# A hybrid attention and gating block on one core: the last query rotation behind the first attention loads, softmax tiles in pools of their own region, an early exponential

## The chip, the cores and the metric

The kernel runs on one core of a Trainium2 chip. The metric is the device time of one execution in microseconds (us); the time of a kernel is the median of its runs. One more execution was recorded by the hardware profiler, and all durations of single instructions are from it. The engines are named as in the profile: PE (TensorE, matrix products), DVE (VectorE), ACT (ScalarE), POOL (GpSimd) and SP (SyncE, which here only issues DMAs). A line number such as L377 is a line of the kernel before.

## The reference

The block has one layer. It normalises x (1024 tokens by 1024 channels), projects it once, and splits the columns into two gated branches; in short:

```python
h = rmsnorm(x, norm_g[l])
q, k, v, za, u, vs, zs, gm = jnp.split(h @ w_in[l], IN_SPLITS, axis=-1)
q = partial_rope(q.reshape(B, S, ATT_HEADS, HEAD_DIM), pos)      # 16 heads of 64, first 16 dims rotated
k = partial_rope(k.reshape(B, S, ATT_KV_HEADS, HEAD_DIM), pos)   # 2 key heads
a = window_sink_attention(q, k, v, att_sinks[l])                 # chunks of 64, window of 3 chunks
a = (a * jax.nn.silu(za)) @ w_att_out[l]
sgo = chunked_spatial_gating(gelu(u), gelu(vs), sg_w[l], sg_b[l], sg_ln_g[l], sg_ln_b[l])
sgo = (sgo * jax.nn.silu(zs)) @ w_sg_out[l]
ga, gs = jnp.split(jax.nn.sigmoid(gm + b_merge[l]), N_BRANCHES, axis=-1)
x = x + (ga * a + gs * sgo) @ w_o[l]
return rmsnorm(x, final_g)
```

Attention takes for each chunk of 64 queries the keys of its own chunk and the two before it. The softmax has one learned sink logit for each head, so the row maximum and the denominator take the sink in.

## The kernel before, in words

All large products run in fp32 by a split of each operand into a high and a low part (fp32r): three products stand for one. A product of two 256-row blocks of output by 1024 columns of tokens is done by a Strassen-like scheme with seven products instead of eight. `gemm_pair` (L351) does one such pair: it takes the forms of the input ("b11", "t1", "t2", "b21", "t3", "b22", "t4") as moving operands and split weights (`ready`) as stationary ones. Each of the seven is a `product` (L334) of 12 matrix instructions of 128x512 at L342. The order in the code is b11, t1, t2, b21, t3, b22, t4. Three banks take the sums: `acc` ("mm") gets b11, t2, t3 and t4 one after the other, so a product with t4 has to wait until the subtraction of L377 has read what t3 left; `t5` ("o") gets t1 and b22.

After each product `gemm_pair` calls a `hook`. Other work is hung on these hooks, a step at a time: that is how attention, rotation and loads come to lie beside the products. `split_next` casts the weights of the next pair on ACT (L155) and takes the rest on DVE (L156); `make_sums` adds weight blocks on DVE (L242 to L245).

The stages that matter here follow one another. Four pairs make the queries q; they go raw to `q_raw` in DRAM (L458) and, scaled and split (`split_q`: ACT L1034, DVE L1036), to `q_hl` by DMAs on SP (L1040). The first 16 of 64 dims of each head have to be rotated: `rotate(g, pause)` (L1083) loads them for eight heads from `q_raw` into tiles "rot" (L1089, four DMAs), multiplies them with tables of cosines and sines on DVE (L1109 to L1116), splits them in tiles "qhl" and stores them to `q_hl` over the plain values (two halves with four DMAs each, L1040). `rope_tables` makes the tables, `rotate_keys` does the same for the keys. `rotate(0, 3)` runs on the hooks of the last query pair, `rotate(1, 1)` on those of the pair after it, the first of the z stage ("z pair").

On the same hooks, behind the rotation, `first_loads` loads keys and queries of the first two attention steps (`query_stage`, L1152 and L1184). Attention itself begins on the first hook of the next pair. There are 32 steps, each of 128 queries by 4 heads. `softmax_stage` (L1212) makes scores on PE (L1230, bank "sc", two of them), row minima on DVE (L1238, L1239; scores carry a negative scale), and exponentials on ACT into a tile "pr" (L1243); the small values lie in tiles "sm". `weight_stage` turns the weights on PE (L1274), `value_stage` multiplies them with the values (L1315). Step 2 of attention loads its queries when the scores of step 0 have been read, as there are two tiles "q".

On-chip memory is taken in pools, stacked. The pool "ahead" is open from before the queries to the end of attention. On it lies "queries" with all tiles of rotation and splitting ("cos", "sin", "wide", "tab", "qhl", "rot"); it is closed behind the z pair, and "attention" with "sm", "pr", "pT", "pTb", "aT" and "vb" takes the same place. A tile of the later pool waits for whatever still uses the place in the earlier one.

The order of instructions on each queue is not that of the code. The framework traces the program, then plans each engine's queue with a cost model of its own; earlier in the code means a higher priority, and an instruction that is ready sooner may go first. `after(second, first)` (L158) adds an order without a wait; `pace[0]` is the last copy that ended a product, `term[0]` the last finished sum. Every queue then runs strictly in the planned order.

The line that hangs up the two jobs is L1197:

```python
steps_of_q += [rotate(1, 1), first_loads()]
gemm_pair(hb, rest(z_dr, 0), part_of_q)
stage.close()
```

Of the kernel before, what the change touches and what calls it, by code (L numbers as in the profile page):

```python
# [24 lines left out]
F32 = mybir.dt.float32  # L25
F32R = mybir.dt.float32r
# [4 lines left out]
P = 128  # L31
# [3 lines left out]
HALF = 512  # L35
# [17 lines left out]
def hybrid_tile(  # L53
# [947 lines left out]
    aheads = ahead.enter_context(tc.tile_pool(name="ahead", bufs=1))  # L1001
    stage = ExitStack()
    pool = stage.enter_context(tc.tile_pool(name="queries", bufs=1))
    SC = -(HD**-0.5)
    tables = []

    def rope_tables():

        cos_sb = mtile([P, NT, 16], F32, "cos", 1, pool)
        sin_sb = mtile([P, NT, 16], F32, "sin", 1, pool)  # L1010
        nc.sync.dma_start(cos_sb[:], cos)
        nc.sync.dma_start(sin_sb[:], sin)
        yield
        for src in (cos_sb[:, :, 0:8], sin_sb[:, :, 8:16]):
            tab = mtile([P, HALF], F32, f"tab{len(tables)}", 1, pool)
            wide = []
            for i in range(4):
                v = mtile([P, 2, 8, 8], F32, "wide", 4, pool)
                nc.vector.tensor_copy(v[:], src[:, i : i + 5 : 4, :].unsqueeze(2).broadcast_to([P, 2, 8, 8]))
                wide.append(v)  # L1020
            yield
            pt = bank("tp")
            for i, v in enumerate(wide):
                nc.tensor.transpose(pt[:, i * P : (i + 1) * P], v[:].rearrange("p a h d -> p (a h d)"), ident[:])
            nc.scalar.copy(tab[:], pt[:])
            tables.append(tab)
            yield

    def split_q(src, places):

        hl = mtile([P, 2, HALF], F32R, "qhl", 3, pool)
        hi, lo = (hl[:, a, :].rearrange("p (t q c) -> p t c q", c=2, q=64) for a in range(2))
        src = src.rearrange("p (t c q) -> p t c q", c=2, q=64)
        nc.scalar.mul(hi, src, SC)  # L1034
        for c in range(2):
            nc.vector.scalar_tensor_tensor(  # L1036
                lo[:, :, c], src[:, :, c], SC, hi[:, :, c].bitcast(F32), op0=ALU.mult, op1=ALU.subtract
            )
        for at, dst in places:
            nc.sync.dma_start(dst, hl[at].bitcast(F32))  # L1040
# [3 lines left out]
    def rotate_keys(pause):  # L1044

        x1, x2, a, b = (mtile([P, HALF], F32, "rot", 5, pool) for _ in range(4))
        for j, dst in enumerate((x1, x2)):
            nc.gpsimd.memset(dst[:], 0.0)  # L1050
            src = k_raw[:].rearrange("(g d) t -> g d t", g=2)[:, 8 * j : 8 * j + 8]
            for half in range(2):
                nc.sync.dma_start(dst[half * 64 : half * 64 + 16], src[:, :, half_of(half)])

        def split_rows(src, j):
            hl = mtile([P, 2, HALF], F32R, "qhl", 3, pool)
            split(hl[:, 0, :], hl[:, 1, :], src)
            for half in range(2):
                for dup in range(2):
                    for g in range(2):  # L1060
                        at = half * 64 + 8 * g
                        nc.gpsimd.dma_start(
                            k_dr[dup * HD + 8 * j : dup * HD + 8 * j + 8, 2 * g : 2 * g + 2, half_of(half)],
                            hl[at : at + 8].bitcast(F32),
                        )

        for _ in range(1 + pause):
            yield
        c, s = tables[0][:], tables[1][:]
        after(nc.vector.tensor_mul(a[:], x1[:], c), term[0])  # L1070
        after(nc.vector.tensor_mul(b[:], x2[:], s), term[0])
        yield
        after(nc.vector.tensor_sub(a[:], a[:], b[:]), term[0])
        split_rows(a[:], 0)
        yield
        after(nc.vector.tensor_mul(x2[:], x2[:], c), term[0])
        after(nc.vector.tensor_mul(x1[:], x1[:], s), term[0])
        yield
        after(nc.vector.tensor_add(x2[:], x2[:], x1[:]), term[0])
        split_rows(x2[:], 1)  # L1080
        yield

    def rotate(g, pause):  # L1083

        x1, x2, a, b = (mtile([P, HALF], F32, "rot", 5, pool) for _ in range(4))
        for j, dst in enumerate((x1, x2)):
            src = q_raw[:].rearrange("(h d) t -> h d t", h=16)[8 * g : 8 * g + 8, 8 * j : 8 * j + 8]
            for half in range(2):
                nc.sync.dma_start(dst[halves[half]], src[:, :, half_of(half)])  # L1089

        def split_rows(src, j):
            split_q(
                src,
                [
                    (
                        (halves[half], a),
                        q_hl[a].rearrange("(h d) t -> h d t", h=16)[
                            8 * g : 8 * g + 8, 8 * j : 8 * j + 8, half_of(half)
                        ],
                    )  # L1100
                    for a in range(2)
                    for half in range(2)
                ],
            )

        for _ in range(1 + pause):
            yield
        c, s = tables[0][:], tables[1][:]
        after(nc.vector.tensor_mul(a[:], x1[:], c), term[0])  # L1109
        after(nc.vector.tensor_mul(b[:], x2[:], s), term[0])  # L1110
        nc.vector.tensor_sub(a[:], a[:], b[:])
        split_rows(a[:], 0)
        yield
        after(nc.vector.tensor_mul(x2[:], x2[:], c), term[0])
        after(nc.vector.tensor_mul(x1[:], x1[:], s), term[0])
        nc.vector.tensor_add(x2[:], x2[:], x1[:])  # L1116
        split_rows(x2[:], 1)
        yield
# [75 lines left out]
            yield  # L1194


    steps_of_q += [rotate(1, 1), first_loads()]  # L1197
    gemm_pair(hb, rest(z_dr, 0), part_of_q)
    stage.close()


    stage = ExitStack()
    pool = stage.enter_context(tc.tile_pool(name="attention", bufs=1))

    def atile(shape, dt, tag, bufs):
        return mtile(shape, dt, tag, bufs, pool)

    def window_of(t, c):

# [2 lines left out]
    def softmax_stage(g, t, par, qt):  # L1212

        kt = keys[g, t][0]
        q_of = qt[:].rearrange("p i (q c) -> p c (i q)", c=2)
        k0 = 0 if t else P
        nmax = atile([P, 2, 2], F32, "sm", 12)
        sums = atile([P, 2, 2], F32, "sm", 12)  # L1220
        pr = atile([P, 2, 384], F32, "pr", 2)
        held_in = {}
        sinks_of = (v[:, 4 * g + par : 4 * g + par + 3 : 2] for v in (sink_sb, nsink_sb))
        sk, nsk = sinks_of
        for c in range(2):
            lo, hi = window_of(t, c)
            sc = bank("sc")[:].rearrange("p (i k) -> p i k", i=2)
            for i in range(2):
                for f in range(2):
                    nc.tensor.matmul(  # L1230
                        sc[:, i, k0:],
                        q_of[:, c, i * P : (i + 1) * P],
                        kt[:, f, k0:],
                        start=f == 0,
                        stop=f == 1,
                    )

            nc.vector.tensor_reduce(nmax[:, c, :], sc[:, :, lo:hi], axis=mybir.AxisListType.X, op=ALU.min)  # L1238
            nc.vector.tensor_tensor(nmax[:, c, :], nmax[:, c, :], nsk, op=ALU.min)  # L1239
            for i in range(2):  # L1240
                at = 192 * c if t else P * (c + 1)
                held_in[c, i] = pr[:, i, at : at + hi - lo]
                nc.scalar.activation(  # L1243
                    held_in[c, i],
                    sc[:, i, lo:hi],
                    AF.Exp,
                    bias=nmax[:, c, i : i + 1],
                    scale=-1.0,
                    accum_out=sums[:, c, i : i + 1],
                )  # L1250
        es = atile([P, 2, 2], F32, "sm", 12)
        nc.vector.tensor_add(es[:], sk.unsqueeze(1).broadcast_to([P, 2, 2]), nmax[:])
        nc.scalar.activation(es[:], es[:], AF.Exp)
        nc.vector.tensor_add(es[:], es[:], sums[:])
        inv = atile([P, 2, 2], F32, "sm", 12)
        nc.vector.reciprocal(inv[:], es[:])
        for c in range(2):
            for i in range(2):
                v = held_in[c, i]
                if c == 0:  # L1260
                    nc.vector.tensor_scalar_mul(v, v, inv[:, c, i : i + 1])
                else:
                    nc.scalar.mul(v, v, inv[:, c, i : i + 1])
        return pr
# [635 lines left out]
```

## Time and profile before

| what | us |
|---|---|
| median of 3 runs | 914.42 |
| lowest and highest | 913.27, 915.49 |
| the profiled execution, as timed | 915.36 |
| its span, first to last instruction | 913.6 |
| PE busy in it | 895.3 |
| DVE, ACT, POOL busy | 696.7, 527.1, 141.9 |

The mean granted clock of PE is 0.995. In rows of a timeline the first number is the start in us from the span's beginning, the second the duration in us (of all instructions that the row merges), then engine, line, operation, tile written and tiles read; in brackets stands how long the engine had been idle before, and what ended that. Rows with a stretch (300.00:320.00) give its length, then for PE, PE's weight loads, DVE, ACT and POOL the busy time and number of instructions, then the granted clock, the DMA engines' share and GB/s. Rows of waits give the sum, the number and the longest. In the chain of waits a row is start, duration and what filled it. "SPq" rows are DMAs being issued, not moved.

### The profile page before, as it was taken

Reading aid. Unit: us, or ns where it says so; the run is one execution under the profiler, and the core shown is the slowest. Engines: PE = TensorE matmul, PEld = TensorE weight load, DVE = VectorE, ACT = ScalarE, POOL = GpSimd, SP = SyncE. Lnnn points to the kernel's source line nnn. Section 1 sums busy time; section 2 is a strip of 40 time slices with the busy share of each in tenths; the row PEclk is TensorE's granted clock in tenths of the full one; section 3 lists DMA queues with packets and bytes.
Section 4 is the critical chain, followed back from the end, with each engine's and each line's share of the span. In section 5 each row is a group of like instructions: output and inputs, shape, how many; then the busy total and the mean of one; then the engine's idle time right before and its main releaser. Section 6 shows DMA issues by size and latency. Waiting matters only on the chain.

```text
span 913.6 us, 13183 instructions
## 1 busy us (share of the span) xinstructions
PE 895.3 (98%) x4284; PEld 745.1 (82%) x4284; DVE 696.7 (76%) x1263; ACT 527.1 (58%) x1058; POOL 141.9 (16%) x204
## 2 busy tenths in 40 slices
PE   8999999999999899999999999999998999999996
PEld 6778888888888788888888888888877887888885
DVE  6869966666685678888878888647797589579996
ACT  6866533334544467677677676664674385367443
POOL 1222222212030001111110111201001111110012
PEclk9999999999999999999999999999999999999999
DMA  9997888958788657878686789899859755998632
GB/s 330 204 248 212 271 203 173 172 158 257 260 258 274 199 167 212 212 153 208 180 227 228 234 240 229 215 338 343 304 195 363 224 201 150 312 304 277 208 117 113
DMA packets 131598, 209.57 MB, mean 229 GB/s; under 512 B 12649, under 2 KB 61033, under 8 KB 131530
## 3 DMA queue, kind: packets, MB, share of 16 engines
q1 hardware_dynamic: 110072, 149.74, 49.7%
q0 software_dynamic: 21312, 58.73, 28.3%
q8 instruction: 34, 0.56, 0.3%
q14 instruction: 34, 0.28, 0.1%
q10 hardware_dynamic: 146, 0.27, 0.1%
HBM read 147.74 MB, written 86.11 MB: 256 GB/s over the span
## 4 chain that ended last, share of the span: by engine, by line
PE 88%; DVE 7%; DMA 2%; issue 1%; ACT 1%; SPq 0%; DVEq 0%; ACTq 0%
PE ps_mm L342 37%; PE ps_o L342 27%; PE ps_sc L1230 3%; PE ps_mm L669 3%; PE ps_tp L342 3%; PE ps_tp L669 2%; PE ps_o L1315 2%; PE ps_sc L342 2%; PE ps_tp L1274 2%; PE ps_o L669 2%; PE ps_tp L917 2%; PE ps_sc L669 1%; DVE bq L185 1%; DVE wl L156 1%; DMA wr<-in_w_dram 1%
## 5 line engine op out<-in xcount | busy, mean ns | idle before, releaser
L155 ACT CAST wh<-s 128x1024 fp32r<-128x1024 f32 (+1 forms) x79 | 79.2, 1005 | 90.2 <-PE ps_mm L342 48.6
L156 DVE TENSOR_TENSOR wl<-wr,wh 128x512 fp32r<-128x512 f32 (+1 forms) x77 | 72.0, 936 | 51.3 <-ACT wh L155 50.7
L156 DVE TENSOR_TENSOR wl<-s,wh 128x1024 fp32r<-128x1024 f32 (+1 forms) x79 | 92.5, 1171 | 10.8 <-ACT wh L155 10.6
L155 ACT CAST wh<-wr 128x512 fp32r<-128x512 f32 (+1 forms) x77 | 63.1, 821 | 62.6 <-PE ps_mm L342 34.2
L342 PE MATMUL ps_o<-T_t1h,wh 128*128 128x512 f32 x148 | 58.9, 398 | 0.8 <-ACT wh L155 0.7
L342 PE MATMUL ps_o<-T_b22h,wh 128*128 128x512 f32 x148 | 58.2, 393 | 0.0
L342 PE MATMUL ps_o<-T_b22l,wh 128*128 128x512 f32 x148 | 57.9, 391 | 0.0
L342 PE MATMUL ps_o<-T_b22h,wl 128*128 128x512 f32 x148 | 57.8, 390 | 0.0
L342 PE MATMUL ps_mm<-T_b11h,wl 128*128 128x512 f32 x140 | 54.9, 392 | 2.8 <-DVE wl L156 2.8
L342 PE MATMUL ps_o<-T_t1h,wl 128*128 128x512 f32 x148 | 57.7, 390 | 0.0
L342 PE MATMUL ps_o<-T_t1l,wh 128*128 128x512 f32 x148 | 57.6, 389 | 0.0
L342 PE MATMUL ps_mm<-T_t4h,wh 128*128 128x512 f32 x140 | 55.5, 397 | 1.2 <-DVE x L377 1.2
L342 PE MATMUL ps_mm<-T_t2h,wl 128*128 128x512 f32 x140 | 55.2, 395 | 0.0
L342 PE MATMUL ps_mm<-T_t3l,wh 128*128 128x512 f32 x140 | 54.6, 390 | 0.6 <-DVE T_t3l L156 0.6
L342 PE MATMUL ps_mm<-T_t2l,wh 128*128 128x512 f32 x140 | 55.2, 394 | 0.0
L342 PE MATMUL ps_mm<-T_t4h,wl 128*128 128x512 f32 x140 | 55.1, 394 | 0.0
L342 PE MATMUL ps_mm<-T_b11h,wh 128*128 128x512 f32 x140 | 55.1, 393 | 0.0
L342 PE MATMUL ps_mm<-T_t4l,wh 128*128 128x512 f32 x140 | 55.0, 393 | 0.0
L342 PE MATMUL ps_mm<-T_t2h,wh 128*128 128x512 f32 x140 | 55.0, 393 | 0.0
L342 PE MATMUL ps_mm<-T_b11l,wh 128*128 128x512 f32 x140 | 54.9, 392 | 0.0
L342 PE MATMUL ps_mm<-T_t3h,wh 128*128 128x512 f32 x140 | 54.9, 392 | 0.0
L1243 ACT ACTIVATE pr<-ps_sc,sm 128x192 f32<-128x192 f32 (+2 forms) x128 | 50.9, 410 | 6.6 <-DVE sm L1239 5.5
(389 smaller groups left out, 2397.4 us busy)
## 6 DMA issues: line engine op xcount, KB each, us to landing
wr<-in_w_dram SPq DMA_DIRECT2D x86, 256.0 KB
sums<-in_w_dram POOLq DMA_DIRECT2D x20, 512.0 KB, 6.5
s<-sums SPq DMA_DIRECT2D x20, 512.0 KB
q_hl<-qhl SPq DMA_DIRECT2D x16, 512.0 KB
q<-q_hl SPq DMA_DIRECT2D x64, 128.0 KB
y_dr<-x POOLq DMA_DIRECT2D x28, 256.0 KB, 6.7
g<-in_w_dram POOLq DMA_DIRECT2D x12, 512.0 KB, 6.7
wr<-in_w_dram SPq DMA_DIRECT2D x11, 512.0 KB
```

The source lines that it names most:

```text
L155: nc.scalar.copy(hi, src)
L156: return nc.vector.tensor_sub(lo, src, hi.bitcast(F32))
L185: op(dst[:, i : i + 2, :], a[:, i : i + 2, :], c[:, i : i + 2, :])
L342: nc.tensor.matmul(acc, lt, rt, start=fresh and k == 0 and n == 0, stop=k == 3 and n == 2, skip_group_check=True,)
L669: mm = nc.tensor.matmul(acc[:], lt, rt, start=fresh and k == 0 and n == 0, stop=k == 3 and n == 2, skip_group_check=True,)
L917: nc.tensor.matmul(pm[:, t * P : (t + 1) * P], xh[:, half * 4 + t, g * P : (g + 1) * P], bias[-1][1][:, g % 4, :], start=True, stop=True,)
L1230: nc.tensor.matmul(sc[:, i, k0:], q_of[:, c, i * P : (i + 1) * P], kt[:, f, k0:], start=f == 0, stop=f == 1,)
L1243: nc.scalar.activation(held_in[c, i], sc[:, i, lo:hi], AF.Exp, bias=nmax[:, c, i : i + 1], scale=-1.0, accum_out=sums[:, c, i : i + 1],)
L1274: nc.tensor.transpose(dst, pr[:, i, block * P : block * P + width], ident[:])
L1315: nc.tensor.matmul(po[:, cs], lt, rt, start=n == 0, stop=n == len(terms) - 1)
```

## The change

Four things change.

1. On the hooks of the z pair `first_loads` comes ahead of `rotate(1, 1)`.
2. An exponential of one column ("warm") is issued ahead of the z pair, ordered behind the last copy of the pair before.
3. The tiles "sm" and every other "pr" move into the pool "ahead"; the others of "pr" go to a pool "weights" that is opened first where "queries" was. The split rows "qhl" get a pool "split" on top of "queries".
4. The cosines, the sines and the spread rows ("wide") that become tables use tiles "rot" (five slots of 128x512) instead of tiles of their own.

```diff
     stage = ExitStack()
     pool = stage.enter_context(tc.tile_pool(name="queries", bufs=1))
+    split_pool = stage.enter_context(tc.tile_pool(name="split", bufs=1))
...
+    def rot_tile():
+        return mtile([P, HALF], F32, "rot", 5, pool)
+
+    both = rot_tile()[:, 0 : 2 * NT * 16].rearrange("p (f t d) -> p f t d", f=2, t=NT)
+
     def rope_tables():
 
-        cos_sb = mtile([P, NT, 16], F32, "cos", 1, pool)
-        sin_sb = mtile([P, NT, 16], F32, "sin", 1, pool)
-        nc.sync.dma_start(cos_sb[:], cos)
-        nc.sync.dma_start(sin_sb[:], sin)
+        for f, src in enumerate((cos, sin)):
+            nc.sync.dma_start(both[:, f], src)
         yield
-        for src in (cos_sb[:, :, 0:8], sin_sb[:, :, 8:16]):
+        for src in (both[:, 0, :, 0:8], both[:, 1, :, 8:16]):
             tab = mtile([P, HALF], F32, f"tab{len(tables)}", 1, pool)
-            wide = []
+            wide = rot_tile()
             for i in range(4):
-                v = mtile([P, 2, 8, 8], F32, "wide", 4, pool)
-                nc.vector.tensor_copy(v[:], src[:, i : i + 5 : 4, :].unsqueeze(2).broadcast_to([P, 2, 8, 8]))
-                wide.append(v)
+                nc.vector.tensor_copy(
+                    wide[:, i * P : (i + 1) * P].rearrange("p (a h d) -> p a h d", a=2, h=8),
+                    src[:, i : i + 5 : 4, :].unsqueeze(2).broadcast_to([P, 2, 8, 8]),
+                )
             yield
             pt = bank("tp")
-            for i, v in enumerate(wide):
-                nc.tensor.transpose(pt[:, i * P : (i + 1) * P], v[:].rearrange("p a h d -> p (a h d)"), ident[:])
+            for i in range(4):
+                nc.tensor.transpose(pt[:, i * P : (i + 1) * P], wide[:, i * P : (i + 1) * P], ident[:])
...
-        hl = mtile([P, 2, HALF], F32R, "qhl", 3, pool)
+        hl = mtile([P, 2, HALF], F32R, "qhl", 3, split_pool)
...
-        x1, x2, a, b = (mtile([P, HALF], F32, "rot", 5, pool) for _ in range(4))
+        x1, x2, a, b = (rot_tile() for _ in range(4))
...
-    steps_of_q += [rotate(1, 1), first_loads()]
+    steps_of_q += [first_loads(), rotate(1, 1)]
+    after(nc.scalar.activation(warm[:], eps_sb[:], AF.Exp), pace[0])
     gemm_pair(hb, rest(z_dr, 0), part_of_q)
     stage.close()
 
 
     stage = ExitStack()
+    weights_pool = stage.enter_context(tc.tile_pool(name="weights", bufs=1))
     pool = stage.enter_context(tc.tile_pool(name="attention", bufs=1))
...
+    n_pr = [0]
+
+    def small():
+        return mtile([P, 2, 2], F32, "sm", 12, aheads)
...
-        nmax = atile([P, 2, 2], F32, "sm", 12)
-        sums = atile([P, 2, 2], F32, "sm", 12)
-        pr = atile([P, 2, 384], F32, "pr", 2)
+        nmax, sums = small(), small()
+        n_pr[0] += 1
+        pr = mtile([P, 2, 384], F32, f"pr{n_pr[0] % 2}", 1, aheads if n_pr[0] % 2 else weights_pool)
...
-        es = atile([P, 2, 2], F32, "sm", 12)
+        es = small()
...
-        inv = atile([P, 2, 2], F32, "sm", 12)
+        inv = small()
```

The same replacements of "qhl" and "rot" are made in `rotate_keys` and `rotate`.

More of the change, by code (lines that the diff above doesn't have):

```diff
@@ L1055, in split_rows @@
         def split_rows(src, j):
-            hl = mtile([P, 2, HALF], F32R, "qhl", 3, pool)
+            hl = mtile([P, 2, HALF], F32R, "qhl", 3, split_pool)
             split(hl[:, 0, :], hl[:, 1, :], src)
@@ L1083, in rotate @@
     def rotate(g, pause):
-        x1, x2, a, b = (mtile([P, HALF], F32, "rot", 5, pool) for _ in range(4))
+        x1, x2, a, b = (rot_tile() for _ in range(4))
         for j, dst in enumerate((x1, x2)):
```

## The prediction

> **What bounds the kernel now.** I read the page first, then the table of TensorE's waits, then the stretches of 20 us.
>
> ```profile
> span 913.6 us, 13183 instructions
> PE 895.3 (98%) x4284; PEld 745.1 (82%) x4284; DVE 696.7 (76%) x1263; ACT 527.1 (58%) x1058; POOL 141.9 (16%) x204
> ```
>
> ```profile
> PE ps_mm L342 <- DVE wl L156: 2.8, 2, 1.7
> ...
> PE ps_sc L1230 <- ACT pr L1243: 1.5, 1, 1.5
> PE ps_mm L342 <- DVE x L377: 1.2, 1, 1.2
> ```
>
> ```profile
> 300.00:320.00 20.00, 17.25 (x76) 13.70 (x75) 13.69 (x35) 9.75 (x28) 0.00 (x0) 0.93 0.70 207
> ...
> 680.00:700.00 20.00, 16.89 (x64) 12.58 (x63) 19.03 (x22) 11.26 (x15) 2.17 (x4) 0.91 0.83 304
> ```
>
> TensorE (PE) is busy 895.3 of 913.6 us, so 18.3 us of waits is all that any reordering can win. The edit touches the stretch 300 to 320: 2.75 us idle there (20.00 less 17.25), and a granted clock of 0.93. Two of the listed waits lie in it, the 1.5 us and the 1.2 us one. The longer of the waits for DVE wl lies in 680 to 700, which the edit does not name. So I argue about these two waits, and about what is late next when they go.
>
> The earlier wait, from the timeline (start, duration, engine, line):
>
> ```profile
> 299.45 0.69 DVE L1109 TENSOR_TENSOR rot<-rot,tab 128x512 f32<-128x512 f32 x1
> 299.53 0.39 PE L342 MATMUL ps_mm<-T_t3h,wl 128*128 128x512 f32 x1
> ...
> 303.60 0.68 DVE L377 TENSOR_TENSOR x<-x,ps_mm 128x512 f32<-128x512 f32 x1
> ...
> 304.20 0.75 DVE L1036 SCALAR_TENSOR_TENSOR qhl<-rot,qhl 128x256 fp32r<-128x256 f32 x2
> ...
> 304.33 0.50 PE L342 MATMUL ps_mm<-T_t4h,wh 128*128 128x512 f32 x1 [1.24 <-DVE x L377]
> ```
>
> The third form's last product ends at 299.92 (299.53 + 0.39). The subtraction that reads it (L377) could start then, but starts at 303.60, because VectorE (DVE) takes the rotation's instructions from L1109 on first. The product with t4 writes the same bank and waits 1.24 us. The stretch of 3 us around it shows VectorE full and PE empty:
>
> ```profile
> 303.00:306.00 3.00, 1.76 (x8) 1.41 (x8) 3.00 (x7) 1.08 (x2) 0.00 (x0) 1.00 0.57 162
> ```
>
> The later wait, where attention begins:
>
> ```profile
> 309.36 1.23 DVE L156 TENSOR_TENSOR wl<-s,wh 128x1024 fp32r<-128x1024 f32 x1 [0.20 <-ACT wh L155]
> 309.45 1.05 PE L1230 MATMUL ps_sc<-k,q 128*128 128x128 f32 x8
> ...
> 312.76 0.62 DVE L1238 TENSOR_REDUCE sm<-ps_sc 128x2 f32<-128x128 f32 x2 [2.18 <-DMA z_dr<-x]
> ...
> 313.46 1.29 SPq L1184 DMA_DIRECT2D q<-q_hl  x2
> ...
> 313.67 1.28 ACT L1243 ACT_TABLE_LOAD   x1 [3.43 <-DMA z_dr<-x]
> ...
> 314.97 0.31 ACT L1243 ACTIVATE pr<-ps_sc,sm 128x64 f32<-128x64 f32 x1
> ...
> 315.72 1.39 PE L1230 MATMUL ps_sc<-k,q 128*128 128x128 f32 x8 [1.49 <-ACT pr L1243]
> ...
> 317.32 0.63 PE L342 MATMUL ps_mm<-T_t2h,wl 128*128 128x512 f32 x1
> ...
> 323.62 0.64 PE L1230 MATMUL ps_sc<-k,q 128*128 128x256 f32 x4
> ```
>
> ```profile
> L1238 DVEq EVENT_SEMAPHORE  x4: 49/50/50, 311.6 to 312.7; - x4
> ```
>
> The first scores are there by 310.5 (309.45 + 1.05). The first row minimum (L1238) starts at 312.76, after VectorE's sequencer has gone through four waiting instructions up to 312.7. The profile names z_dr as releaser, but L1238 reads scores and writes a tile "sm" of the pool "attention", which takes the place of "queries"; there lie the split rows "qhl", still read by eight stores to q_hl, issued until 308.97 (row below). A store there takes about 3.9 us to land, hence 312.7. I take these stores as the true releaser. Then ScalarE (ACT) loads the exponential's table, 1.30 us to its first exponential (314.97 less 313.67), and the second group of scores, which needs a bank back, waits 1.49 us.
>
> The wait costs more than itself:
>
> ```profile
> 317.00:319.00 2.00, 2.00 (x6) 1.54 (x6) 1.10 (x7) 2.00 (x11) 0.00 (x0) 0.53 0.62 134
> 319.00:321.00 2.00, 2.00 (x9) 1.58 (x8) 0.99 (x5) 0.92 (x4) 0.00 (x0) 0.62 0.85 236
> ...
> 694.00:696.00 2.00, 2.00 (x7) 1.52 (x6) 2.00 (x3) 0.00 (x0) 1.08 (x2) 0.50 1.08 395
> ```
>
> ```profile
> 285.78 3.89 DMA q_hl<-qhl
> ...
> 291.72 5.90 DMA wr<-in_w_dram
> ...
> 317.11 3.40 PE ps_mm L342 x8
> 320.51 0.51 PE ps_tp L1274 x4
> ...
> 324.73 2.73 PE ps_mm L342 x12
> 327.46 0.44 PE ps_tp L1274 x4
> ```
>
> Behind it the granted clock is 0.53 and 0.62; in the chain of waits eight products take 3.40 us where twelve take 2.73 later. The same dip stands at 694 to 696, behind the other large wait; none follows the 1.24 us one (clock 1.00 in 303 to 306).
>
> **The change part by part.**
>
> Softmax tiles by region. "sm" and the first step's "pr" move into the pool "ahead", which is open beforehand, and the second step's "pr" takes the front of "queries", where "rot" lies and no store reads. So L1238 no longer waits for stores. Its new start is where VectorE is free: in the profile the last split before it ends at 310.59 (309.36 + 1.23). From L1238's start to ScalarE's 0.91 us (313.67 less 312.76), from the first exponential to the second scores 0.75 (315.72 less 314.97): scores at 310.59 + 0.91 + 0.75 = 312.25. PE gets there at 315.72 less both waits, 312.99. The wait of 1.49 goes, with 0.74 to spare.
>
> The dummy exponential. It moves a load of 1.28 us to behind the copy that ends a product of the pair before.
>
> ```profile
> 277.97 1.05 ACT L155 CAST wh<-wr 128x1024 fp32r<-128x1024 f32 x1 [1.61 <-PE ps_o L342]
> ```
>
> ScalarE idles 1.61 us there; load and a tiny exponential are 1.28 + 0.31 = 1.59. I cost it at nothing. Without that cover it is up to 1.59 us on ScalarE, below zero nothing.
>
> The last quarter behind the first loads. The hooks of the z pair now give the two query stages first, then the rotation's loads (third), a pause, and its two halves (fifth and sixth, instead of third and fourth). Its arithmetic stays: six instructions like L1109 and four of L1036. They are ordered behind the latest finished term, and by the fifth hook that is L377: L377 can start at about 300.7 (behind one split of 1.23 us, like L156 above, begun at 299.45 in L1109's place) and end by 301.4, while t4 is due at 303.09 (304.33 less 1.24). The 1.24 us go. On SP:
>
> ```profile
> 291.72 0.60 SPq L200 DMA_DIRECT2D wr<-in_w_dram  x1
> 293.64 2.86 SPq L1089 DMA_DIRECT2D rot<-q_raw  x4
> 296.55 0.62 SPq L1184 DMA_DIRECT2D q<-q_hl  x1
> ...
> 299.93 1.93 SPq L1184 DMA_DIRECT2D q<-q_hl  x3
> ...
> 303.81 5.16 SPq L1040 DMA_DIRECT2D q_hl<-qhl  x8
> ```
>
> Four query loads (0.62 + 1.93 = 2.55 us of issue) go ahead of the four rotation loads. SP stood from 292.32 to 293.64, so these come at most 2.55 − 1.32 = 1.2 us later, and the last lands by about 301.6 (296.5 + 1.2 + 3.9), when VectorE has just done L377. The eight stores stay at 5.16 us and come no earlier than before.
>
> Tables and "split" pool. The cosines, sines and spread rows use "rot" slots; the same copies and transposes remain.
>
> ```profile
> L1025 ACT COPY tab<-ps_tp x2: 587/588/588, 237.2 to 242.8; 128x512 f32<-128x512 f32 x2
> ...
> L1070 DVE TENSOR_TENSOR rot<-rot,tab x1: 687/687/687, 246.2 to 246.2; 128x512 f32<-128x512 f32 x1
> ```
>
> The key rotation's first product (246.2) may now wait for these slots, free by 243.4 (242.8 + 0.59): nothing, with 2.8 us to spare.
>
> The sum: waits 1.24 + 1.49; the eight slow products 3.40 − 8/12 × 2.73 = 1.58; the slow scores 1.39 − 1.05 = 0.34; the slow transposes 0.51 − 0.44 = 0.07. Together 4.72 us. The profiled execution took 915.36 us (span 913.6) and would take 910.6; the median of the three runs shown is 914.42, 0.94 lower, so 909.7.
>
> Here one rule speaks against the sum. The row: a wait of 1.49 us, then a clock of 0.53. The Trainium skill (TensorE: Matmul & The Clock Gate, "What's actually happening") has the half rate only after an idle window of some 3.4 us. By that rule the dip is not this wait's, and the sum would be 2.73 us. The trace disagrees, with a dip directly behind each of the two large waits, and I sum by the trace.
>
> What I cannot see is the order: the framework plans every queue anew from its own costs (loads written after the eight stores were issued before them, 296.55 against 303.81). The later waits at 680 to 700 may shift either way by their size; I take zero.
>
> **The rivals.**
>
> The third step's queries are late next. Their loads are issued at 313.46 and about 314.1, and land 3.89 to 5.90 us later, 318.0 to 320.0. PE takes these scores at 323.62 now, but would at 323.62 − 4.72 = 318.9. For it: SP issues without a pause from 303.81. Against: four loads have left that stretch. It gives back up to 1.1 us, and with a dip like the one above (1.58 + 0.34 + 0.07 = 1.99) 3.1: 910.8 to 912.8.
>
> VectorE's order. The rotation now stands right ahead of the first row minimum, and the spare is 0.74 us. For it: L377 stood 3.7 us behind just these instructions. If they run 1.5 us or more late, a wait of 0.8 to 1.4 and the dip come back: 912.5 to 913.1. The same page of the Trainium skill ("Architectural detail: the array is 16× 32×32, not 1× 128×128") says that ACT and DVE are strict first-in first-out; L377 agrees.
>
> The clock dips anyway, by the idle-window rule's reading that something else causes it: only 1.24 + 1.49 come, 911.7. Against it speaks the place of both dips.
>
> The change does nothing: "sm" still waits for the region it left, or the dummy is planned late; 914.4. Against: nothing in "ahead" is read by those stores.
>
> Slower: the rotation, two products of 2.73 later, takes its eight stores along, 5.5 us. The third step's query loads stand behind them on SP: issued by 319.6, landed by 323.5 to 325.5, against 318.9 due. A wait of 4.6 to 6.6 and the dip of 1.99 outweigh 4.72: 916.3 to 918.3. It decides where the loads land after 318.9 + 2.7 = 321.6. Against: the rotation began late before too (299.45), for its data.
>
> **How the numbers follow.** Chances: forecast 0.42 (909.7), third queries 0.22 (about 911.8), VectorE's order 0.12 (912.8), dip anyway 0.05 (911.7), nothing 0.06 (914.4), slower 0.13 (917). A measurement here can tell about 0.2%, 1.8 us, from no change: faster means below 912.6. That is the forecast 0.42, most of the third queries 0.20, a quarter of VectorE's order 0.03 and the dip 0.05: 0.70. The rest of those two, 0.11, and nothing, 0.06, make 0.17. Slower 0.13. The range runs from 908.6 (the sum and about one of the later waits) to 915.5, which leaves out most of the slower case.
>
> **What would show it.** Right: L377 within 1.5 us of the third form's last product and no wait at t4; L1238 without waiting instructions; the table load near 276 to 290; clock 1.00 from 300 to 325. The rivals: a wait of L1230 on q's DMA at the third step; L1238 more than 2 us behind its scores with VectorE busy; the eight stores past 312. The forecast is wrong if PE's idle time before 330 does not fall by 2 us.

## The result, and the profile after

The changed kernel takes 911.88 us in the median of 12 runs (910.54 to 913.13), the kernel before 914.25 us in 12 runs beside them: a ratio of 0.998 with a 95% interval of 0.9971 to 0.9989. Two later comparisons gave 911.77 against 914.74 us (0.9965, 0.9952 to 0.9979) and 912.0 against 915.15 us (0.9966, 0.9954 to 0.9978). So the medians differ by 2.4 to 3.2 us, and the ratios say 1.8 to 3.2. The forecast was 4.7: the kernel got faster, but by about half of that. The profiled execution of the changed kernel took 912.14 us, that of before 915.36.

In the lines of after, L1242 are the scores (L1230 before), L1250 the row minimum (L1238), L1255 the exponential (L1243), L1114 to L1121 the rotation, L1045 the stores to q_hl, L1189 the query loads, L1203 the dummy exponential. First the page and TensorE's waits of after:

```profile
span 910.4 us, 13184 instructions
PE 894.2 (98%) x4284; PEld 743.6 (82%) x4284; DVE 696.8 (77%) x1263; ACT 527.0 (58%) x1059; POOL 141.9 (16%) x204
```

```profile
PE ps_mm L342 <- DVE wl L156: 2.9, 2, 1.8
...
PE ps_mm L342 <- ACT x L360: 0.6, 1, 0.6
PE ps_sc L1242 <- ACT pr L1255: 0.4, 1, 0.4
```

Both waits that the prediction summed are gone from this list. In their place stand two short ones, 0.6 and 0.4 us (the columns of waits are sum, number and longest). The waits for wl, which the change does not touch, are as they were. The stretches of 20 and 2 us that showed the loss before now read:

```profile
300.00:320.00 20.00, 19.61 (x95) 15.89 (x94) 16.44 (x40) 10.81 (x33) 0.00 (x0) 1.00 0.70 211
317.00:319.00 2.00, 2.00 (x13) 1.70 (x12) 1.09 (x4) 1.83 (x5) 0.00 (x0) 1.00 0.92 257
319.00:321.00 2.00, 2.00 (x14) 1.81 (x13) 2.00 (x5) 1.33 (x3) 0.00 (x0) 1.00 0.94 219
680.00:700.00 20.00, 17.54 (x70) 13.75 (x69) 16.75 (x19) 8.81 (x12) 2.17 (x4) 0.91 0.90 330
```

From 300 to 320 TensorE is idle for 0.39 us instead of 2.75, and the granted clock is 1.00 throughout. The timeline of after shows the new order:

```profile
277.36 1.28 ACT L1203 ACT_TABLE_LOAD   x1
278.65 0.20 ACT L1203 ACTIVATE warm<-eps_sb 128x1 f32<-128x1 f32 x1
...
302.32 0.68 DVE L377 TENSOR_TENSOR x<-x,ps_mm 128x512 f32<-128x512 f32 x1
...
303.05 0.50 PE L342 MATMUL ps_mm<-T_t4h,wh 128*128 128x512 f32 x1
...
303.52 0.68 DVE L1114 TENSOR_TENSOR rot<-rot,tab 128x512 f32<-128x512 f32 x1
...
307.88 5.50 SPq L1045 DMA_DIRECT2D q_hl<-qhl  x8
...
310.67 0.75 DVE L1041 SCALAR_TENSOR_TENSOR qhl<-rot,qhl 128x256 fp32r<-128x256 f32 x2
311.34 0.61 DVE L1250 TENSOR_REDUCE sm<-ps_sc 128x2 f32<-128x128 f32 x2
...
312.12 0.31 ACT L1255 ACTIVATE pr<-ps_sc,sm 128x64 f32<-128x64 f32 x1 [1.78 <-DVE sm L1251]
...
312.87 1.39 PE L1242 MATMUL ps_sc<-k,q 128*128 128x128 f32 x8 [0.38 <-ACT pr L1255]
...
314.32 3.21 SPq L1189 DMA_DIRECT2D q<-q_hl  x4
...
320.09 1.11 PE L1242 MATMUL ps_sc<-k,q 128*128 128x256 f32 x8
```

The subtraction L377 comes ahead of the rotation (L1114), and the product with t4 follows it. The eight stores are issued some 4 us later than before (303.81 then), yet the row minimum does not wait for them: it follows directly on VectorE's last split.

### The profile page after: what moved, and what is told of

It is laid out like the page before. It is cut to its first block, busy times and chain, and to the rows that moved or that the text cites. A ratio compares the mean times of both kernels' runs of the same rounds, so it can differ in the third digit from the quotient of the medians.

```text
span 910.4 us, 13184 instructions
## 1 busy us (share of the span) xinstructions
PE 894.2 (98%) x4284; PEld 743.6 (82%) x4284; DVE 696.8 (77%) x1263; ACT 527.0 (58%) x1059; POOL 141.9 (16%) x204
## 4 chain that ended last, share of the span: by engine, by line
PE 87%; DVE 7%; DMA 2%; issue 1%; ACT 1%; SPq 0%; POOL 0%; DVEq 0%; ACTq 0%
PE ps_mm L342 36%; PE ps_o L342 26%; PE ps_sc L1242 3%; PE ps_tp L342 3%; PE ps_mm L669 3%; PE ps_tp L669 2%; PE ps_o L1327 2%; PE ps_sc L342 2%; PE ps_tp L1286 2%; PE ps_o L669 2%; PE ps_tp L917 2%; PE ps_sc L669 1%; DVE wl L156 1%; DVE bq L185 1%; DMA q_hl<-qhl 1%
## 5 line engine op out<-in xcount | busy, mean ns | idle before, releaser
L342 PE MATMUL ps_o<-T_t1h,wh 128*128 128x512 f32 x148 | 58.8, 397 | 0.8 <-ACT wh L155 0.7
L342 PE MATMUL ps_o<-T_b22h,wh 128*128 128x512 f32 x148 | 58.3, 394 | 0.0
L342 PE MATMUL ps_mm<-T_b11h,wl 128*128 128x512 f32 x140 | 55.4, 396 | 2.9 <-DVE wl L156 2.9
L342 PE MATMUL ps_o<-T_b22l,wh 128*128 128x512 f32 x148 | 57.9, 391 | 0.0
L342 PE MATMUL ps_o<-T_b22h,wl 128*128 128x512 f32 x148 | 57.7, 390 | 0.0
L342 PE MATMUL ps_o<-T_t1h,wl 128*128 128x512 f32 x148 | 57.7, 390 | 0.0
L342 PE MATMUL ps_o<-T_t1l,wh 128*128 128x512 f32 x148 | 57.6, 389 | 0.0
L1255 ACT ACTIVATE pr<-ps_sc,sm 128x192 f32<-128x192 f32 (+2 forms) x128 | 50.9, 410 | 9.0 <-DVE sm L1251 6.6
L342 PE MATMUL ps_mm<-T_b11h,wh 128*128 128x512 f32 x140 | 55.3, 395 | 0.0
L342 PE MATMUL ps_mm<-T_t4h,wh 128*128 128x512 f32 x140 | 55.3, 395 | 0.0
L342 PE MATMUL ps_mm<-T_t2h,wh 128*128 128x512 f32 x140 | 54.7, 391 | 0.6 <-ACT x L360 0.6
L342 PE MATMUL ps_mm<-T_t3l,wh 128*128 128x512 f32 x140 | 54.6, 390 | 0.6 <-DVE T_t3l L156 0.6
L342 PE MATMUL ps_mm<-T_b11l,wh 128*128 128x512 f32 x140 | 55.2, 394 | 0.0
L342 PE MATMUL ps_mm<-T_t3h,wh 128*128 128x512 f32 x140 | 54.9, 392 | 0.0
L342 PE MATMUL ps_mm<-T_t4h,wl 128*128 128x512 f32 x140 | 54.7, 391 | 0.0
L342 PE MATMUL ps_mm<-T_t3h,wl 128*128 128x512 f32 x140 | 54.7, 390 | 0.0
L342 PE MATMUL ps_mm<-T_t2h,wl 128*128 128x512 f32 x140 | 54.6, 390 | 0.0
L342 PE MATMUL ps_mm<-T_t2l,wh 128*128 128x512 f32 x140 | 54.6, 390 | 0.0
```

Of the source, the lines that this page charges most:

```text
L342: nc.tensor.matmul(acc, lt, rt, start=fresh and k == 0 and n == 0, stop=k == 3 and n == 2, skip_group_check=True,)
L1255: nc.scalar.activation(held_in[c, i], sc[:, i, lo:hi], AF.Exp, bias=nmax[:, c, i : i + 1], scale=-1.0, accum_out=sums[:, c, i : i + 1],)
```

## The experiments

To compare records I use one stretch: from the first product with t3 at 297.04 us in the record of before to the first product with b11 at 334.53. It holds the same 120 products at L342 in every kernel, so its length shows what the region of the change costs, apart from the scatter of the stages ahead of it. Every median was taken beside runs of the kernel before: 914.03 us beside the kernels with one part and "pools, order", 915.15 beside the other two pairs and the third record of after, 914.74 beside the second. The new tiles of tables and rotation (point 4 of the change) and the pool "split" go with the pools in all of these kernels; no run has them alone.

| kernel | stretch, us | wait at t4 | wait at 2nd scores | half clock in it | median, ratio (95%) |
|---|---|---|---|---|---|
| before | 37.49 | 1.24 | 1.49 | 3.41 | see above |
| before, again | 35.67 | 0.93 | 1.57 | none | 911.6 (one run) |
| pools only | 37.37 | 2.97 | none | 3.41 | 914.42, 0.9998 (0.9987–1.001) |
| dummy only | 36.28 | 1.69 | 1.43 | none | 913.56, 0.9988 (0.9977–0.9999) |
| order only | 38.21 | none | 2.20 | 6.83 | 914.98, 1.0006 (0.9991–1.0021) |
| pools, order | 34.81 | none | 1.20 | none | 913.70, 0.9994 (0.9981–1.0006) |
| pools, dummy | 36.54 | 2.24 | none | 3.41 | 914.06, 0.9986 (0.9974–0.9997) |
| order, dummy | 38.17 | none | 2.52 | 6.83 | 915.02, 1.0006 (0.9994–1.0018) |
| after | 33.41 | none | 0.38 | none | see above |
| after, again | 32.95 | none | none | none | 911.77, 0.9965 |
| after, third | 33.73 | 0.20 | 0.37 | none | 912.0, 0.9966 |

**One part alone.** The pools without the other two (in the changed kernel the order is put back and the dummy left out):

```diff
-    steps_of_q += [first_loads(), rotate(1, 1)]
-    after(nc.scalar.activation(warm[:], eps_sb[:], AF.Exp), pace[0])
+    steps_of_q += [rotate(1, 1), first_loads()]
```

> The pools and the tables of the change alone, rotation first as before, no early exponential. Theory A (the stores held the first row minimum): the minimum starts at about 310.6 instead of 312.76, the table load follows, 310.6 + 0.91 + 1.28 + 0.75 = 313.5, and PE asks at 314.2, so the second wait and the dip go (3.5 us), the 1.24 us wait at t4 stays: about 910.8. Rival B (the table load is what holds the second scores): the wait stays at 1.3 us or more with its dip, about 914. Rival C (the recorded execution of the kernel before was a bad one, other executions lose less there): the waits go as in A, but the timed gain is half of that, about 912.5.

The dummy alone is one line more in the kernel before, the order alone is its one line changed:

```diff
+    after(nc.scalar.activation(warm[:], eps_sb[:], AF.Exp), pace[0])
```

> The early exponential alone. Theory A: the first minimum still waits for the stores until 312.8, but its exponentials start 1.28 us earlier, so the second scores can start at about 314.4 against 314.2: wait 0.2 us, no dip, 3.3 us gained, about 911.0. Rival B (table load) says the same here. Rival C: half of it, about 912.6. If the exponential is planned badly, up to 1.6 us slower elsewhere.

```diff
-    steps_of_q += [rotate(1, 1), first_loads()]
+    steps_of_q += [first_loads(), rotate(1, 1)]
```

> First loads ahead of the rotation, alone. Theory A: the 1.24 us wait at t4 goes, but the rotation's stores land some 4 us later (317 in the changed kernel) and the first row minimum waits for them in the old pool: second wait about 7 us with its dip, about 918 to 919. Rival D (the order alone is what helps, the stores do not hold the minimum): 1.2 us gained, about 913.

Where the expectations above take a wait at its length in the kernel before, the runs miss them: the waits changed with each plan (2.97, 1.69 and 2.20 us). Pools alone gain nothing. The timeline shows why: the rotation still stands ahead of L377, and L377 starts at 305.35, later than before (303.60). TensorE, held up there, makes the first scores at 312.58 only (309.45 before), so the row minimum starts at 313.44 and not at the 310.6 of theory A; it does go right behind VectorE's last split, without waiting instructions, and the second scores do not wait.

```profile
300.21 0.69 DVE L1114 TENSOR_TENSOR rot<-rot,tab 128x512 f32<-128x512 f32 x1 [0.42 <-DMA rot<-q_raw]
...
305.35 0.68 DVE L377 TENSOR_TENSOR x<-x,ps_mm 128x512 f32<-128x512 f32 x1
...
306.09 0.60 PE L342 MATMUL ps_mm<-T_t4h,wh 128*128 128x512 f32 x1 [2.97 <-DVE x L377]
```

With the dummy alone both waits stay (1.69 and 1.43 us); it gains about 0.1%, and the runs do not tell where that comes from. The order alone gains nothing. The instruction rows of L1238 (engine queue, instruction, count, shortest, median and longest in ns, first and last start) and the timeline:

```profile
L1238 DVEq EVENT_SEMAPHORE  x4: 21/50/50, 316.3 to 317.3; - x4
```

```profile
310.49 2.63 SPq L1040 DMA_DIRECT2D q_hl<-qhl  x4
...
317.35 0.62 DVE L1238 TENSOR_REDUCE sm<-ps_sc 128x2 f32<-128x128 f32 x2 [6.09 <-PE ps_o L342]
...
318.18 1.28 ACT L1243 ACT_TABLE_LOAD   x1 [2.35 <-DMA q<-q_hl]
...
320.23 1.97 PE L1230 MATMUL ps_sc<-k,q 128*128 128x128 f32 x8 [2.20 <-ACT pr L1243]
```

The rotation comes later, and so do its stores: the last is issued by 313.12 (308.97 before), and the minimum's waiting instructions end at 317.3 (312.7 before). Both moved by 4 to 5 us together. Together with the kernels that have both the order and the pools, where the stores are as late and the minimum does not wait, that shows the stores to be what it waits for, whatever the profile names in the bracket: the releaser there is PE's ps_o, and in the kernel before it was z_dr.

**Two parts of three.** The changed kernel without the dummy:

```diff
-    after(nc.scalar.activation(warm[:], eps_sb[:], AF.Exp), pace[0])
```

> The whole change without the early exponential. Theory A: the first minimum at 311.3 as in the changed kernel, then the table load of 1.28 us, so the second scores wait 0.4 + 1.28 = 1.7 us and the clock dips (2 us): 3.3 us above the changed kernel, about 915. Without a dip 913.2. Rival D: the early exponential costs ScalarE as much as it saves: equal to the changed kernel, 911.9.

The minimum starts early (312.05), but the table load stands between it and the first exponential, and the second scores wait, 1.20 us and not the 1.7 of theory A, and without a half-clock stretch behind them. In these lines L1241 are the scores and L1254 the exponential:

```profile
312.82 1.28 ACT L1254 ACT_TABLE_LOAD   x1 [1.77 <-DVE sm L1250]
...
314.86 1.38 PE L1241 MATMUL ps_sc<-k,q 128*128 128x128 f32 x8 [1.20 <-ACT pr L1254]
```

The changed kernel with the old order:

```diff
-    steps_of_q += [first_loads(), rotate(1, 1)]
+    steps_of_q += [rotate(1, 1), first_loads()]
```

> The changed kernel with the rotation ahead of the query stages again, as before: the new pools and the dummy exponential stay. Theory A (the new order is what removes the wait at the last product with t4; pools and dummy remove the one at the second scores): the wait at t4 is back, 0.9 to 3.0 us, the one at the second scores is not, under 0.4 us. So the stretch that the changed kernel crosses in 33.0 to 33.4 us takes 34 to 36 us, 1.7 more with a half-clock stretch in it; median 912.6 to 914.3. Rival (the order is worth nothing once the pools are there): within 0.6 us of the changed kernel.

As theory A had it: the wait at t4 is back with 2.24 us, the one at the second scores is not; 914.06 us.

The kernel before with the new order and the dummy:

```diff
-    steps_of_q += [rotate(1, 1), first_loads()]
+    steps_of_q += [first_loads(), rotate(1, 1)]
+    after(nc.scalar.activation(warm[:], eps_sb[:], AF.Exp), pace[0])
```

> The kernel before with the new order and the dummy exponential, without the new pools. Theory A (softmax tiles in the region of the split rows wait for the eight stores, and the new order moves these stores some 4 us back): no wait at t4; the first row minimum starts at 316.5 to 317.8 behind waiting instructions, as with the order alone (317.35); the exponential follows without a table load, so the wait of 2.20 us at the second scores shrinks to 0.7 to 1.3; median 912.6 to 914.6. Rival (the wait was the table's, not the stores'): the minimum starts before 313 and the kernel equals the changed one within 0.5 us.

Here L1231 are the scores, L1239 the row minimum and L1244 the exponential.

```profile
L1239 DVEq EVENT_SEMAPHORE  x4: 21/49/49, 316.8 to 317.6; - x4
```

```profile
317.70 0.62 DVE L1239 TENSOR_REDUCE sm<-ps_sc 128x2 f32<-128x128 f32 x2 [6.28 <-DMA q<-q_hl]
...
318.55 0.31 ACT L1244 ACTIVATE pr<-ps_sc,sm 128x64 f32<-128x64 f32 x1 [2.38 <-DVE sm L1240]
...
319.30 1.97 PE L1231 MATMUL ps_sc<-k,q 128*128 128x128 f32 x8 [2.52 <-ACT pr L1244]
```

The minimum starts at 317.70, as the stores let it, which speaks for theory A. The size of the wait was missed: without the table load the second scores start 0.93 us earlier than with the order alone (319.30 against 320.23), but TensorE gets there 1.25 us earlier (316.78 against 318.03), so the wait is 2.52 us and not 0.7 to 1.3. TensorE's place changes because every edit makes the framework plan the queues anew: between the first and the second scores it puts 16 products of L342 in the kernel before, 38 with the order alone, 31 here, and 12 in the changed kernel. Each part thus uncovers what the next one removes; only the three together take away both waits.

**The same two kernels again.** The kernel before, unchanged:

> The kernel before, unchanged, recorded once more. Theory A (the half-clock stretch at 317 comes in some executions only; the waits always): the waits of TensorE at the last product with t4 (1.0 to 1.7 us) and at the second scores (1.4 to 1.6 us) are there again; half-clock stretches at about 693 and 911 again, and one at 317 or none at all. With it the time is near 915.5, without it near 913.7, since one stretch of 3.4 us at half speed costs 1.7 us. Theory B (the prediction's: the stretch belongs to the 1.49 us wait): wherever that wait stands, the stretch stands behind it, and the time moves for other reasons.

```profile
PE ps_sc L1230 <- ACT pr L1243: 1.6, 1, 1.6
PE ps_mm L342 <- DVE x L377: 0.9, 1, 0.9
```

```profile
315.09 1.39 PE L1230 MATMUL ps_sc<-k,q 128*128 128x128 f32 x8 [1.57 <-ACT pr L1243]
```

```profile
317.00:319.00 2.00, 2.00 (x12) 1.66 (x12) 0.96 (x6) 2.00 (x12) 0.00 (x0) 1.00 0.63 151
```

Both waits are there, together 2.50 us, and the clock behind them is 1.00. So the half clock at 317 need not follow the wait, as theory A said. The one at 694 is gone as well in this record, behind waits of the same length. The stretch takes 1.82 us less than in the first record of the same kernel.

The changed kernel, unchanged, twice:

> The changed kernel, unchanged, recorded once more and timed beside the others. Theory A: no wait at the last product with t4, 0 to 0.6 us at the second scores, no half clock from 300 to 330, median 911.5 to 912.3 and 1.5 to 2.5 us under before. On the 0.57 us stall at 272.4: if it is the plan (a ScalarE queue behind a slot of the split rows that a store holds), it is there again within 0.3 us; if it was one late landing of that store, the gap is under 0.2 us.

> The changed kernel once more, beside the others on the same chip. Median 911.4 to 912.2; no wait at t4; half clock nowhere from 300 to 330; a stall at 272 or 312 of under 0.6 us or none, as its two records had (0.57 and 0.38 us in one, none in the other).

The stretch takes 32.95 and 33.73 us. The stall of 0.57 us at 272 is in neither record, so it does not belong to the plan; a late landing of the store is the likely reason. In the first record of after it reads:

```profile
271.22 1.22 ACT L1039 ACTIVATE qhl<-x 128x512 fp32r<-128x512 f32 x2 [2.93 <-DMA q_hl<-qhl]
272.32 0.56 ACT L360 COPY x<-ps_mm 128x512 f32<-128x512 f32 x1
...
272.94 0.50 PE L342 MATMUL ps_mm<-T_t2h,wh 128*128 128x512 f32 x1 [0.57 <-ACT x L360]
```

There two casts wait for a slot of "qhl" that a store still reads, and the copy that frees TensorE's bank stands behind them on ScalarE. In the other two records the same casts wait there too (1.70 and 1.77 us), but the copy comes in time.

**When the half clock comes.** Every record ends in a half-clock stretch, behind a window in which TensorE is idle for 3.28 to 3.41 us. Ten records have others, and in each of them the starts of the stretches, the last one's too, lie whole multiples of 3.4133 us apart (110.00, 64.00, 109.00, 113.00, 176.00, 173.00 and so on). So these windows run on a grid of their own whose place against the span is chance. Below, each pair of rows shows one such window and the next (busy TensorE is the first number behind the comma, the granted clock the third from the end): pools only, pools and dummy, dummy only, before again, and before.

```profile
302.92:306.33 3.41, 0.44 (x2) 0.25 (x2) 3.39 (x7) 0.67 (x1) 0.00 (x0) 1.00 0.56 143
306.33:309.74 3.41, 3.41 (x9) 2.66 (x9) 3.41 (x9) 1.73 (x2) 0.00 (x0) 0.50 0.44 139
```

```profile
303.13:306.54 3.41, 1.17 (x5) 0.86 (x5) 3.41 (x7) 0.67 (x1) 0.00 (x0) 1.00 0.62 152
306.54:309.95 3.41, 3.41 (x9) 2.63 (x8) 3.41 (x7) 1.72 (x2) 0.00 (x0) 0.50 0.49 163
```

```profile
301.74:305.15 3.41, 1.72 (x8) 1.13 (x7) 3.41 (x7) 0.67 (x1) 0.00 (x0) 1.00 0.60 160
305.15:308.56 3.41, 3.41 (x16) 2.81 (x16) 3.41 (x8) 2.09 (x3) 0.00 (x0) 1.00 0.47 153
```

```profile
312.04:315.45 3.41, 1.84 (x10) 1.26 (x9) 0.98 (x5) 2.40 (x8) 0.00 (x0) 1.00 0.87 271
315.45:318.86 3.41, 3.40 (x20) 2.85 (x20) 1.93 (x12) 3.39 (x16) 0.00 (x0) 1.00 0.78 187
```

```profile
313.69:317.10 3.41, 1.91 (x12) 1.34 (x11) 0.66 (x5) 3.38 (x12) 0.00 (x0) 1.00 0.98 273
317.10:320.51 3.41, 3.41 (x10) 2.53 (x9) 1.76 (x10) 2.33 (x12) 0.00 (x0) 0.50 0.68 168
```

Over all 14 records, from 200 us on and without the end of the span, every window with 1.89 us or more of idle TensorE (11 of them) is followed by a half-clock window, and of nine between 1.50 and 1.75 two are, both in the record of before. With less idle than that only two are, and both are half-clock windows themselves, the first of the two joined ones that the order alone and order with dummy have. In the last pair above, the window also holds scores of 1.39 us at 128 columns, and such short products may count as partly idle. The records bear that out: in L342's products of 128x512 alone this window is busy for 0.69 us, and the two half-clock windows that another one follows for 0.95 and 1.40. From 200 us on, 13 of the 14 windows with under 1.5 us of these wide products are followed by half clock, and of those with more only two (1.52 and 1.67 us; four others at 1.67 are not). This is a count over the records at hand; no run varied the short products. The Trainium skill (TensorE: Matmul & The Clock Gate, "What's actually happening") states this free-running window of 3413 ns; the grid agrees with it. It has the half rate after an idle window, and there the traces differ: 1.89 idle of 3.41 us is enough.

**Four slots for the split rows.** The changed kernel with four slots "qhl" (in both places that take one); one rotation tile and one "pr" make room for them. Its control has the room made, and three slots:

```diff
-        return mtile([P, HALF], F32, "rot", 5, pool)
+        return mtile([P, HALF], F32, "rot", 4, pool)
...
-        hl = mtile([P, 2, HALF], F32R, "qhl", 3, split_pool)
+        hl = mtile([P, 2, HALF], F32R, "qhl", 4, split_pool)
...
-        pr = mtile([P, 2, 384], F32, f"pr{n_pr[0] % 2}", 1, aheads if n_pr[0] % 2 else weights_pool)
+        pr = mtile([P, 2, 384], F32, f"pr{n_pr[0] % 2}", 1, weights_pool)
```

The control (three slots):

> The changed kernel with four slots for the rotation's rows instead of five, and both probability tiles in the front of the region they leave. It is the control for the next kernel. If five slots matter nowhere: the changed kernel's time within 0.7 us, 911.2 to 912.6. If a rotation's tile has to wait for the slot that the tables held, TensorE gets a new wait at 237 to 260 and the time is 1 us or more above.

Four slots, timed twice:

> The kernel rot4 with four slots for the split rows instead of three, which the room of one rotation tile and one probability tile pays for. Theory A (0.9 us were lost at 272 because a ScalarE cast waits for a slot that a store of 5 to 6 us holds, and 0.4 us at the second scores because the rotation's last splits stand ahead of the first minimum): the copy of the product at 270.7 to 271.3 starts as in the kernel before, no stall at 272, and since its VectorE order has the first minimum ahead of the last split, no wait at the second scores; 0.5 to 1.3 us under rot4, 910.6 to 911.5. Rival (the stall was chance, and the order costs nothing): within 0.4 us of rot4.

> The changed kernel with four slots for the split rows, four for the rotation's rows and both probability tiles in the region they leave, once more. If the small gain is real: 0.3 to 1.2 us under the changed kernel of the same call. If it was chance: within 0.3 us.

The control takes 912.21 us (0.9975, 0.9966 to 0.9984), with a wait of 0.54 us at the second scores. With four slots it is 911.16 us (0.9959, 0.9945 to 0.9973) and 910.69 us (0.9955, 0.9939 to 0.9971), 0.6 and 1.3 us under the changed kernel beside it. Nothing of this comes from 272, where the control has no stall. VectorE's order has changed: the first half of the first minimum goes ahead of the rotation's last split, and the second scores wait for 0 and 0.13 us in the two records.

```profile
309.87 0.29 DVE L1250 TENSOR_REDUCE sm<-ps_sc 128x2 f32<-128x128 f32 x1
...
310.69 0.76 DVE L1041 SCALAR_TENSOR_TENSOR qhl<-rot,qhl 128x256 fp32r<-128x256 f32 x2 [0.33 <-ACT qhl L1039]
...
312.62 1.22 PE L1242 MATMUL ps_sc<-k,q 128*128 128x128 f32 x8
```

This version is faster than the kernel before. Over the changed kernel a gain is not shown: the intervals overlap, and so do the stretches (32.54 and 33.23 us against 32.95 to 33.73). The runs without a half-clock stretch ahead of the end (a mean clock of 0.998, see below) have a mean of 910.45 us here and 910.51 with the changed kernel. More of this version's runs are of that kind, 6 of 11 against 9 of 32, and whether that is more than chance its 11 runs do not tell.

## Why the prediction was right in direction and wrong in size

**The first wait (1.24 us): right.** L377 comes ahead of the rotation and the wait goes; kernels that keep the old order show it with 0.93 to 2.97 us. L377 starts at 302.32, 1.6 us later than forecast, because more of VectorE's other work goes ahead of it. That is 1.86 us behind the third form's last product, more than the 1.5 that the prediction named as a sign of being right, and little was to spare: one record waits 0.20 us.

**The second wait (1.49 us): right in its mechanism.** The stores to q_hl were the true releaser, and the minimum no longer has waiting instructions. But it starts at 311.34 and not 310.59, as the rotation's last split stands ahead of it, so the second scores can start at 312.87 and not at 312.25. And TensorE, with 12 products behind the first scores instead of 16, gets there at 312.49 and not at 312.99. These 0.62 and 0.50 us eat the spare of 0.74, and 0.38 us are left as a wait (0.37 and 0 in the other two records). That is the rival of VectorE's order in less than half of its size and without a dip.

**The dip (1.99 us): the step that failed.** The prediction took both places where a dip stood behind a large wait for a rule, and summed the whole dip as if every execution had it. It comes in some only. The granted clock that is listed with each run tells how often. In the 14 records a mean clock of 0.998 goes with no half-clock window ahead of the span's end, 0.996 with one of 3.41 us, 0.995 or 0.994 with two, apart or joined, and 0.992 with three. The 82 runs of before whose clock is listed split so: 11 runs at 0.998 with a mean of 912.40 us, 22 at 0.996 with 914.10, 40 at 0.995 and 0.994 with 915.8 (nine at 0.997 fit neither side). One stretch thus costs 1.7 us, which is half of 3.41. Of the 32 runs of the changed kernel 9 are at 0.998 with a mean of 910.51, 16 at 0.996 with 912.44, six at 0.997, and one is below. On average the change has some 0.7 stretches fewer (1.4 of before less 0.7, without the runs at 0.997), so an estimate of what the dips gave is 1.1 us, where the prediction put 1.99.

The size of one dip was off as well: 0.34 of the 1.99 us are not the clock's. The prediction took the second scores' 1.39 us for slowed ones, but they take 1.39 us at full clock too, in after and in the second record of before, and in the first they end at 317.11, where the slow stretch begins. And its bound of 18.3 us counted slow products as busy time, so it was no bound on what a dip can give.

The rival "the clock dips anyway" (911.7 us, chance 0.05) has the number of what came, 911.88, and so has that of the late queries (911.8); both are luck. The first had the whole 2.73 us of the waits and no dip, the second a new wait that did not come. What came is 1.8 us of waits and 1.1 of dips, about the 2.8 us between the two means, 914.68 and 911.87. The prediction kept the whole dip on two sightings in one execution. It also made the sum against an execution with two such windows, 0.94 us over the median, and subtracted that difference again, although part of the dip was in it.

**The waits (2.73 us): a term that was too large by as much.** At an equal number of stretches the change gains 1.9 and 1.7 us (912.40 less 910.51, 914.10 less 912.44). TensorE's idle time ahead of 330 us agrees: 6.39 and 5.82 us in the two records of before, 4.32, 4.37 and 4.12 in the three of after, so it falls by 1.45 to 2.27 us (2.07 between the first two records); the prediction called itself wrong below 2. The two waits add up to only 2.50 us in the second record of before, and short new ones come in some records of after: up to 0.38 us at the second scores, 0.20 at t4, 0.57 at 272. Another 0.2 to 0.5 us are lost in attention: from the product with b11 that ends the stretch to the last product with t2 before the waits near 680, all records with the new pools take 341.14 to 341.19 us and those with the old ones 340.65 to 340.94. TensorE has no pause of over 0.1 us there, so it is no single wait, and its cause stays open. The stages before add scatter: their products with t3 start between 296.63 and 298.83 us in records of these two kernels.

**The dummy at nothing, the loads, the tables: right.** The table load lies at 277.36, behind the copy that ends a product, and no wait of TensorE follows from it. Without the dummy 1.20 us stand at the second scores. The third step's scores start at 320.09 without a wait, so the rival of late queries did not come. Nor did the slower one, although its sign did: the stores end at 313.38, past 312. The query loads behind them are issued from 314.32 to 317.53 (before: from 313.46), not by 319.6, so they were pushed back by 0.86 us only. The later waits stayed (the longest 1.75 us against 1.74), as taken.

## What to carry to other kernels

Look at which tiles share memory with buffers that stores still read; a later store there delays the first write of the next stage, whatever the profile names as releaser. Parts of a change that clear a chain of waits have to be judged together: here each alone, and each pair, was worth at most 0.14%. Before a slow-clock stretch is put into a sum, find out from several executions how often it comes: the same wait came with it and without. The same goes for comparing two kernels: compare runs with the same number of such stretches.

## What the runs showed of the hardware that was not expected

The clock's windows of 3.413 us run on a grid that is fixed within an execution and falls differently in each. The same waits near 680 to 692 us (0.63 to 0.64, 0.67 to 0.74 and 1.74 to 1.75 us in all records) brought a half-clock window in eight of 14 records and none in six. From 200 us on, a window with 1.89 us or more of idle was always followed by one at half clock, and waits of 2.20 and 2.52 us at the second scores, with the short products behind them, by two in a row (6.83 us). So a longer wait can cost more than itself: the stretch with a wait of 1.20 us and no half clock takes 34.81 us, that with 2.52 us and two such windows 38.17.
